# Two halves of a sparse attention result stored apart, and keys turned by DMA, in a one-core hybrid decoder layer

## The chip, the cores and the metric

The kernel runs on one core of a Trainium2 chip. The metric is the device time of one execution in microseconds (us); lower is better. A core has a matrix engine (PE, with its weight loader PEld), a vector engine (DVE), an engine for activations and copies (ACT), a general engine (POOL) and a queue (SP) from which this kernel issues all its transfers. Engines run side by side, each through its own instructions in order, and meet at semaphores.

## The reference, cut to what matters

One decoder layer over 1024 tokens of width 1024, float32:

```python
h = x @ w_in                                   # queries, keys, values, gates of both groups
o_diff = diff_attention(dq, dk, dv, ...)       # 4 heads, two softmaxes each, subtracted; RMS norm per head
o_nsa = gates[0]*o_cmp + gates[1]*o_sel + gates[2]*o_win   # 8 heads, sparse: compressed, selected, window
mix = concat([o_diff, o_nsa], -1) @ w_out
x = layer_norm(ALPHA * x + mix)
x = layer_norm(ALPHA * x + (silu(x @ w_gate) * (x @ w_up)) @ w_down)
```

Columns 0 to 511 of the concatenated row come from the differential heads, columns 512 to 1023 from the sparse heads.

## The kernel before

A float32 operand is kept as two tiles, a rounded part (hi) and a remainder (lo), and a product is three matmuls (`mm3`, L116 to L118). `split` (L81, L83) makes the pair: ACT copies, then DVE or POOL subtracts.

**Order of the work.** After the inputs and the first projections, attention runs in ten phases. A phase has units (a query block of 128 tokens of a pair of sparse heads, or of one differential head) and fillers (projections of the next queries, keys and values, and the first rows of the output projection) that are pumped between the units' steps. A unit has a `front` (scores with `scores`, L323 to L332; exponentials with `exps`, L346; gates on POOL, L411) and a `back` (transposes on PE, copies of them by ACT and DVE, products with the values into the one bank psO). The tile framework turns this into one fixed instruction order for each engine, the SP queue included, by priorities and modelled durations; it also adds the semaphores and gives out buffers: five tiles of the tag `w`, two banks psS, three psT, two psM, one psO.

**The end of a sparse unit.** For a block `i` and a head pair `p`, the selected and the window kind add into the same psO bank. Its upper 64 partitions hold the product with the values' hi, its lower 64 that with the values' lo. At the end of the window kind ACT copies the lower 64 to `tmp` (L433), DVE adds the upper 64 (L434), and two transfers (L436) store the two heads' 64x128 results to `mix_d[i]`, columns 4 to 7 of its eight column blocks. There are 32 such ends.

**Keys.** `k_fill` loads a 1024x128 weight, projects one half of the tokens at a time into a psM bank, and `evac_k` empties it: for each of the two heads in the bank, ACT writes hi to one half of the partitions (L170) and DVE writes lo to the other half (L171). This happens for ten halves beside attention, and for two halves ahead of it, from a psT bank. Queries are emptied by `evac_q` (L176, L177), after which three transfers inside SBUF (`move`, L161) copy partition halves.

**The output projection.** `out_start(i)` loads the residual row and the mix row `mix_d[i]`: `load_split_here` loads the sparse half (columns 512 to 1023) first, then the differential half, each to where lo will stand, and splits it (ACT, then DVE for rows 0 to 3, POOL for rows 4 to 7). A row takes two `w` tiles. `out_half` multiplies the sparse columns first, 24 matmuls for each half row and 48 in all; L605 adds the residual. Rows 0 to 3 are fillers of the last two phases; rows 4 to 7 stand behind attention, beside transposes (`x_put`, L913) for the feed-forward part, which takes the rest of the time and is not touched.

Of the kernel before, what the change touches and what calls it, by code (L numbers as in the profile page):

```python
# [11 lines left out]
F32 = mybir.dt.float32  # L12
# [5 lines left out]
P = 128  # L18
T = 1024
DM = 1024  # L20
NB = T // P
KT = DM // P
# [15 lines left out]
def layer_kernel(ctx: ExitStack, tc: tile.TileContext, xT, x, w_t, w_vg, w_dv, lam_in, subln,  # L38
# [4 lines left out]
    nc = tc.nc  # L43
# [5 lines left out]
    dram = ctx.enter_context(tc.tile_pool(name="dram", bufs=1, space=bass.MemoryType.DRAM))  # L49
# [7 lines left out]
    def ps_o():  # L57
        return psum.tile([P, 512], F32, tag="O", name="psO", bufs=1)
# [10 lines left out]
    def w_tile(dt=F32R):  # L69

        return slots.tile([P, 1024], dt, tag="w", name="w", bufs=5)

    mix_d = dram.tile([NB, P, KT, P], F32, name="mix_d")
    wo_d = dram.tile([2, 4, P, 1024], F32, name="wo_d")
    x1_d = dram.tile([NB, P, DM], F32, name="x1_d")
    a_d = dram.tile([NF // 2, 7, P, 512], F32, name="a_d")
# [2 lines left out]
    def split(src, hi, lo, l_eng="dve"):  # L79

        nc.scalar.copy(hi, src)  # L81
        eng = nc.vector if l_eng == "dve" else nc.gpsimd
        eng.tensor_sub(lo, src, hi.bitcast(F32))  # L83
# [9 lines left out]

    def load_split_here(src, hi, lo, l_eng="dve", order=(0,)):

        n = 1024 // len(order)
        for k in order:
            raw = lo[:, k * n:(k + 1) * n].bitcast(F32)
            nc.sync.dma_start(raw, src[:, k * n:(k + 1) * n])
            split(raw, hi[:, k * n:(k + 1) * n], lo[:, k * n:(k + 1) * n], l_eng)  # L100
        return hi, lo

    def w_tiles():
        lo = w_tile()
        return w_tile(), lo
# [38 lines left out]
    with ExitStack() as ctx_a:  # L144
        pa = ctx_a.enter_context(tc.tile_pool(name="pa", bufs=1))

        def small(shape, tag, bufs, dt=F32):
            return pa.tile(shape, dt, tag=tag, name=tag, bufs=bufs)
# [9 lines left out]
                    yield 0.33  # L158

        def move(dst, src):  # L160
            nc.sync.dma_start(dst.bitcast(F32), src.bitcast(F32))  # L161

        def evac_k(out):

            def f(hf, ps):
                cs = slice(hf * 512, (hf + 1) * 512)
                for g in range(2):
                    own = slice(g * 64, g * 64 + 64)
                    other = slice(64 - g * 64, 128 - g * 64)
                    nc.scalar.copy(out[g][own, cs], ps[own])  # L170
                    nc.vector.tensor_sub(out[g][other, cs], ps[own], out[g][own, cs].bitcast(F32))  # L171
            return f

        def evac_q(q, scale, ps):
# [120 lines left out]
        def q_of(qt, i, a):  # L295

            q = qt[1 + i // 4][a]
            c = (i % 4) * P
            return q[:, c:c + P], q[:, 512 + c:512 + c + P]
# [38 lines left out]
        def t_tiles(width):  # L338

            if width <= 512:  # L340
                t = pa.tile([P, 1024], F32, tag="t", name="t", bufs=6)
                return [t[:, 0:512], t[:, 512:1024]]
            return [pa.tile([P, 1024], F32, tag="t", name="t", bufs=6) for _ in range(2)]
# [31 lines left out]
        def nsa_units(p, qt, K, V):  # L375


            g = p // 2
            heads = (2 * p, 2 * p + 1)
            sl = [SLOPES[4 + h] for h in heads]  # L380
            state = {}

            def make(i, kind):
                nb = i + 1 if kind == 0 else min(i + 1, WIN_BLOCKS)
                j0 = i + 1 - nb
                width = nb * P
                ts = []

                def front():
                    dist = dsel[:, 1024 - width:] if kind == 0 else dwin[:, 640 - width:]  # L390
                    m = small([P, 4], "m", 4)
                    r = small([P, 4], "r", 4)
                    ts.extend(t_tiles(width))
                    if kind == 0:
                        pc = pa.tile([P, 2, NC], F32, tag="pc", name="pc", bufs=3)
                        ts.append(pc)
                    for a in range(2):
                        ms, rs = ([t[:, n:n + 1] for n in (a, 2 + a)] for t in (m, r))
                        cmp = (pc[:, a, :], dcmp[:, 56 - 8 * i:56 - 8 * i + NC], ms[1]) if kind == 0 else None
                        scores(q_of(qt, i, a), K[kind], j0 * P, width, dist, sl[a], ms[0], ts[a], cmp)  # L400
                        exps(ts[a], width, ms[0], rs[0])
                        if kind == 0:
                            exps(pc[:, a, :], NC, ms[1], rs[1])
                    nr = 2 if kind else 4
                    nc.vector.reciprocal(r[:, :nr], r[:, :nr])  # L405
                    for a in range(2):
                        for n, t in ((1 + kind, ts[a][:, :width]), (0, pc[:, a, :] if kind == 0 else None)):
                            if t is not None:
                                gc = heads[a] * 3 + n
                                c = a if n else 2 + a  # L410
                                nc.gpsimd.tensor_scalar(t, t, r[:, c:c + 1], gates[:, i, gc:gc + 1],  # L411
                                                        op0=ALU.mult, op1=ALU.mult)

                def back(fill):
                    if kind == 0:
                        state["po"] = po = ps_o()
                        ptc = transposed([ts[2][:, a, :] for a in range(2)], rows=64)
                        nc.tensor.matmul(po[:, :256], lhsT=vcc[g], rhs=ptc[:, 0, :256], start=True, stop=False)
                    po = state["po"]
                    for jj in range(0, nb, 2):  # L420
                        js = range(jj, min(jj + 2, nb))
                        pt = transposed([ts[a][:, j * P:(j + 1) * P] for j in js for a in range(2)])
                        for n, j in enumerate(js):
                            v = V[kind][:, (j0 + j) * P:(j0 + j + 1) * P]
                            last = kind == 1 and j == nb - 1
                            nc.tensor.matmul(po[:, :256], lhsT=v, rhs=pt[:, 0, n * 256:(n + 1) * 256],  # L426
                                             start=False, stop=False)
                            nc.tensor.matmul(po[:, :256], lhsT=v, rhs=pt[:, 1, n * 256:(n + 1) * 256],  # L428
                                             start=False, stop=last)
                        fill((jj + len(js)) / nb)  # L430
                    if kind == 1:
                        tmp = small([P, 256], "tmp", 3)[0:64, :]
                        nc.scalar.copy(tmp, po[64:128, :256])  # L433
                        nc.vector.tensor_add(tmp, po[0:64, :256], tmp)  # L434
                        for a in range(2):
                            nc.sync.dma_start(mix_d[i, a * 64:(a + 1) * 64, 4 + p, :], tmp[:, a * P:(a + 1) * P])  # L436

                return front, back, 2.0 * nb + 1

            return [make(i, kind) for i in range(NB) for kind in range(2)]  # L440
# [75 lines left out]
        def proj_steps(w, hf, done):  # L516

            ps = ps_m()
            for k in range(KT):
                ks = slice(k * P, (k + 1) * P)  # L520
                proj_mm3(ps, w[0][:, ks], w[1][:, ks], *x_at(k, hf * 512, 512), k == 0, k == KT - 1)
                yield 0.65
            done(hf, ps)

        def k_fill(n, where, out, halves=(0, 1)):
            def steps():
                if 0 in halves:
                    out.extend([slot(m) for m in where])
                    out.append(load_split(w_t[n], *w_tiles(), l_eng="pool", pieces=2))
                for hf in halves:  # L530
                    yield from proj_steps(out[2], hf, evac_k(out))
                    there.add((n, hf))
            return steps, 5.2 * len(halves)

# [52 lines left out]
        mix_rows = {}  # L587

        def out_start(i):

            acc[i] = slot((8, 9, 10, 11, 4, 2, 3, 5)[i], F32)
            nc.sync.dma_start(acc[i], x[i * P:(i + 1) * P, :])
            mix_rows[i] = load_split_here(mix_d[i].rearrange("p k t -> p (k t)"), *w_tiles(),
                                           "dve" if i < 4 else "pool", order=(1, 0))

        def out_half(i, nh, ps):
            m = mix_rows[i]
# [121 lines left out]
        for k0, nk in ((0, 3), (3, 3), (6, 2)):  # L719
            n = nk * 280  # L720
# [340 lines left out]
    for p in range(NF // 2):  # L1061
        f = 2 * p
        g = [gate_tile() for _ in range(2)]
        gate, up = gate_up(f, w_gate, f, half_tile(0)), gate_up(f + 1, w_up, f, half_tile(1))
# [129 lines left out]
    for j in range(4):  # L1194

        n = 2 if j == 3 else 1
        for c in range(n):
            cs = slice(c * 512 // n, (c + 1) * 512 // n)
# [5 lines left out]
            dst = acc[j + 4][:, cs]  # L1204
# [66 lines left out]
```

## Time and profile before

| | |
|---|---|
| median of 3 runs | 1304.74 us (1304.59 to 1304.9) |
| profiled execution, its own time | 1305.84 us |
| its span, first to last instruction | 1304.1 us |
| granted PE clock | 0.999 |
| transfers | 183.13 MB, mean 140 GB/s |

The 1.74 us between the profiled execution's time and its span lie outside the instructions. In the profile, "L434" is a line of the kernel; a row of a group gives engine, operation, what is written and read, shapes, the count, the busy time and the mean in ns. A PE matmul of 512 columns is shown for about 390 ns, but the next one starts about 230 ns later: matmuls overlap, and a full PE row hides waits of up to some 160 ns.

### The profile page before, as it was taken

To read this page: it belongs to the slowest core of one execution; us is meant where nothing else is said; L and a number is where in the kernel's file an instruction comes from. 1 tells how busy PE (TensorE), PEld (TensorE's weight loads), DVE (VectorE), ACT (ScalarE), POOL (GpSimd) and SP (SyncE) were. 2 spreads that over 40 slices of the span, in tenths; PEclk is the share of its full clock that TensorE was granted. 3 is DMA by queue.
4 is the path that set the end of the run, shared out by engine and by line. 5 is a ranking of instruction groups with operands and counts; after the bars stand their busy time and mean duration, and the time that the engine had idled before them with its cause. 6 is when DMAs were issued, how large, how long until landed. Compare 5 with 4: busy or idle time off the path is not lost.

```text
span 1304.1 us, 20490 instructions
## 1 busy us (share of the span) xinstructions
PE 1286.2 (99%) x6955; PEld 1107.8 (85%) x6955; DVE 917.8 (70%) x1963; ACT 652.1 (50%) x1398; POOL 464.1 (36%) x499
## 2 busy tenths in 40 slices
PE   9999999999999999999999999999999999999997
PEld 7998999988988889788887888888888888888886
DVE  5567867778778667774797677776766768555588
ACT  5366866868776566653353333333333335533330
POOL 4434534545435446643613313232231222000071
PEclk9999999999999999999999999999999999999999
DMA  9412012121112135623224566555555559768641
GB/s 354 132 31 62 22 35 62 49 48 48 35 55 70 50 94 149 218 82 113 81 76 149 180 232 228 194 178 173 174 170 185 187 179 346 259 200 291 195 168 65
DMA packets 86841, 183.13 MB, mean 140 GB/s; under 512 B 10576, under 2 KB 19152, under 8 KB 86608
## 3 DMA queue, kind: packets, MB, share of 16 engines
q1 hardware_dynamic: 86736, 181.82, 42.7%
q8 instruction: 55, 0.90, 0.3%
q14 instruction: 50, 0.41, 0.1%
HBM read 116.18 MB, written 57.15 MB: 133 GB/s over the span
## 4 chain that ended last, share of the span: by engine, by line
PE 91%; DVE 4%; DMA 2%; ACT 2%; issue 1%; POOL 0%; SPq 0%; DVEq 0%; ACTq 0%
PE psM L116 11%; PE psM L118 11%; PE psM L117 11%; PE psS L118 6%; PE psS L117 6%; PE psS L116 6%; PE psT L118 5%; PE psT L117 5%; PE psT L116 5%; PE psT L365 4%; PE psS L323 3%; PE psS L326 3%; PE psO L428 2%; PE psO L426 2%; PE psO L481 2%; PE psO L116 2%
## 5 line engine op out<-in xcount | busy, mean ns | idle before, releaser
L346 ACT ACTIVATE t<-t,m 128x384 f32<-128x384 f32 (+7 forms) x192 | 144.2, 752 | 65.4 <-DVE m L332 59.8
L411 POOL TENSOR_SCALAR t<-t,r,gates 128x640 f32<-128x640 f32 (+7 forms) x128 | 99.6, 783 | 180.5 <-DVE r L405 82.4
L116 PE MATMUL psM<-big,w 128*128 128x512 f32 x304 | 120.6, 397 | 0.6 <-DVE slot L171 0.3
L118 PE MATMUL psM<-big,w 128*128 128x512 f32 x304 | 120.1, 396 | 0.0
L117 PE MATMUL psM<-big,w 128*128 128x512 f32 x304 | 119.9, 394 | 0.0
L323 PE MATMUL psS<-slot,q 128*128 128x320 f32 (+10 forms) x304 | 111.8, 369 | 2.2 <-DVE m L332 2.0
L1019 POOL TENSOR_TENSOR half<-half,half 128x512 f32<-128x512 f32 x22 | 33.5, 1524 | 205.0 <-ACT half L1018 205.0
L83 DVE TENSOR_TENSOR pt<-psT,pt 128x512 fp32r<-128x512 f32 (+1 forms) x152 | 91.3, 615 | 13.1 <-ACT pt L81 11.7
L326 PE MATMUL psS<-slot,q 128*128 128x320 f32 (+10 forms) x304 | 99.5, 329 | 0.0
L81 ACT CAST pt<-psT 128x512 fp32r<-128x512 f32 (+1 forms) x152 | 77.3, 525 | 20.6 <-PE psT L365 10.0
L81 ACT CAST big<-slot 128x1024 fp32r<-128x1024 f32 (+1 forms) x54 | 54.4, 1018 | 66.2 <-DVE slot L1011 50.5
L83 DVE TENSOR_TENSOR op<-op 128x1024 fp32r<-128x1024 f32 x44 | 60.9, 1388 | 36.3 <-ACT op L81 35.8
L83 DVE TENSOR_TENSOR big<-slot,big 128x1024 fp32r<-128x1024 f32 (+1 forms) x54 | 63.5, 1182 | 30.5 <-ACT big L81 30.3
L365 PE MATMUL psT<-ident,t 128*128 128x128 f32 x528 | 83.8, 273 | 0.8 <-DVE pt L83 0.7
L81 ACT CAST op<-op 128x1024 fp32r<-128x1024 f32 x44 | 45.9, 1052 | 61.8 <-DMA op<-t_d 55.6
L428 PE MATMUL psO<-pt,slot 128*128 128x256 f32 x264 | 72.1, 294 | 0.1
L426 PE MATMUL psO<-pt,slot 128*128 128x256 f32 x264 | 71.8, 289 | 0.0
L332 DVE CUSTOM_DVE_ANT_0 t<-psS,dsel 128x384 f32<-128x384 f32 (+9 forms) x128 | 62.3, 493 | 13.4 <-PE psS L326 9.6
L1023 POOL TENSOR_TENSOR half<-half,half 128x512 f32<-128x512 f32 x22 | 36.5, 1659 | 99.0 <-DVE half L1022 98.8
L81 ACT CAST big<-big 128x1024 fp32r<-128x1024 f32 (+1 forms) x49 | 44.2, 912 | 45.6 <-DMA big<-t_d 34.0
L118 PEld LDWEIGHTS psM<-big,w 128*128 128x128 f32 x304 | 57.1, 188 | 11.4
L116 PEld LDWEIGHTS psM<-big,w 128*128 128x128 f32 x304 | 57.2, 188 | 11.1 <-ACT w L81 0.8
(371 smaller groups left out, 3971.3 us busy)
## 6 DMA issues: line engine op xcount, KB each, us to landing
a_d<-slot SPq DMA_DIRECT2D x77, 256.0 KB, 3.0
t_d<-slot SPq DMA_DIRECT2D x77, 256.0 KB, 2.2
q<-q SPq DMA_DIRECT2D x48, 256.0 KB, 2.9
slot<-in_w_up_dram SPq DMA_DIRECT2D x22, 512.0 KB, 3.8
slot<-in_w_down_dram SPq DMA_DIRECT2D x22, 512.0 KB, 3.9
op<-a_d SPq DMA_DIRECT2D x44, 256.0 KB, 3.5
op<-t_d SPq DMA_DIRECT2D x44, 256.0 KB, 4.0
big<-a_d SPq DMA_DIRECT2D x33, 256.0 KB, 2.9
```

Of the source, the lines that this page charges most:

```text
L81: nc.scalar.copy(hi, src)
L83: eng.tensor_sub(lo, src, hi.bitcast(F32))
L116: nc.tensor.matmul(acc, lhsT=ah, rhs=bh, start=first, stop=False, skip_group_check=more)
L117: nc.tensor.matmul(acc, lhsT=ah, rhs=bl, start=False, stop=False, skip_group_check=more)
L118: nc.tensor.matmul(acc, lhsT=al, rhs=bh, start=False, stop=last, skip_group_check=more)
L323: mm = nc.tensor.matmul(ps[:, :c + part], lhsT=q[0], rhs=k[:, ks], start=True, stop=False)
L326: nc.tensor.matmul(ps[:, :c + part], lhsT=q[1], rhs=k[:, ks], start=False, stop=True)
L346: nc.scalar.activation(t[:, :width], t[:, :width], AF.Exp, bias=m, scale=-1.0, accum_out=r)
L365: nc.tensor.transpose(tp[:rows, n * P:(n + 1) * P], s, ident)
L411: nc.gpsimd.tensor_scalar(t, t, r[:, c:c + 1], gates[:, i, gc:gc + 1], op0=ALU.mult, op1=ALU.mult)
L426: nc.tensor.matmul(po[:, :256], lhsT=v, rhs=pt[:, 0, n * 256:(n + 1) * 256], start=False, stop=False)
L428: nc.tensor.matmul(po[:, :256], lhsT=v, rhs=pt[:, 1, n * 256:(n + 1) * 256], start=False, stop=last)
```

## The change

Three edits.

1. At the end of a sparse unit ACT copies the whole psO bank (128 partitions) to `tmp`. The add is gone from this place. Two transfers store the two partition halves to a new DRAM tensor `mixs_d[i, n]`, one for the hi part and one for the lo part, each with both heads.
2. `out_start` loads the two stored halves into the two halves of a third `w` tile, adds them on POOL, and splits the sum into hi and lo. The differential half is loaded and split as before, from a `mix_d` that now has only four column blocks.
3. For keys beside attention, ACT copies the whole psM bank to the hi tile and DVE subtracts to the lo tile, 128 partitions each. Then three transfers exchange a quarter of each through a DRAM tensor `turn_d`, so that each head has its hi and its lo in one tile. The two halves ahead of attention keep `evac_k`.

```diff
-    mix_d = dram.tile([NB, P, KT, P], F32, name="mix_d")
+    mix_d = dram.tile([NB, P, 4, P], F32, name="mix_d")
+    mixs_d = dram.tile([NB, 2, P, 4, P], F32, name="mixs_d")
+    turn_d = dram.tile([5, 2, 64, 512], F32, name="turn_d")
...
+        def evac_k_whole(out, n):
+
+            def f(hf, ps):
+                cs = slice(hf * 512, (hf + 1) * 512)
+                nc.scalar.copy(out[0][:, cs], ps)
+                nc.vector.tensor_sub(out[1][:, cs], ps, out[0][:, cs].bitcast(F32))
+                up, down = out[1][0:64, cs], out[0][64:128, cs]
+                move(turn_d[n, hf], down)
+                move(down, up)
+                move(up, turn_d[n, hf])
+            return f
...
                     if kind == 1:
-                        tmp = small([P, 256], "tmp", 3)[0:64, :]
-                        nc.scalar.copy(tmp, po[64:128, :256])
-                        nc.vector.tensor_add(tmp, po[0:64, :256], tmp)
-                        for a in range(2):
-                            nc.sync.dma_start(mix_d[i, a * 64:(a + 1) * 64, 4 + p, :], tmp[:, a * P:(a + 1) * P])
+                        tmp = small([P, 256], "tmp", 3)
+                        nc.scalar.copy(tmp, po[:, :256])
+                        for n in range(2):
+                            nc.sync.dma_start(mixs_d[i, n, :, p, :].rearrange("(a e) t -> e a t", a=2),
+                                              tmp[n * 64:(n + 1) * 64, :].rearrange("e (a t) -> e a t", a=2))
...
-                    yield from proj_steps(out[2], hf, evac_k(out))
+                    yield from proj_steps(out[2], hf, evac_k_whole(out, (n - 9) // 2 if n > 3 else 4))
...
-            mix_rows[i] = load_split_here(mix_d[i].rearrange("p k t -> p (k t)"), *w_tiles(),
-                                           "dve" if i < 4 else "pool", order=(1, 0))
+            raw, m, l_eng = w_tile(F32), w_tiles(), "dve" if i < 4 else "pool"
+            parts = [raw[:, n * 512:(n + 1) * 512] for n in range(2)]
+            for n in range(2):
+                nc.sync.dma_start(parts[n], mixs_d[i, n].rearrange("p k t -> p (k t)"))
+            nc.gpsimd.tensor_add(parts[0], parts[0], parts[1])
+            split(parts[0], m[0][:, 512:1024], m[1][:, 512:1024], l_eng)
+            load_split_here(mix_d[i].rearrange("p k t -> p (k t)"), m[0][:, 0:512], m[1][:, 0:512], l_eng)
+            mix_rows[i] = m
```

More of the change, by code (lines that the diff above doesn't have):

```diff
@@ L94, in load_split_here @@
     def load_split_here(src, hi, lo, l_eng="dve", order=(0,)):
-        n = 1024 // len(order)
+        n = src.shape[-1] // len(order)
         for k in order:
@@ L160, in move @@
         def move(dst, src):
-            nc.sync.dma_start(dst.bitcast(F32), src.bitcast(F32))
+            nc.sync.dma_start(*(t if t.dtype == F32 else t.bitcast(F32) for t in (dst, src)))
         def evac_k(out):
```

## The prediction

> **What bounds the kernel now.** First the page: engine totals and the chain that ended last.
>
> ```profile
> span 1304.1 us, 20490 instructions
> PE 1286.2 (99%) x6955; PEld 1107.8 (85%) x6955; DVE 917.8 (70%) x1963; ACT 652.1 (50%) x1398; POOL 464.1 (36%) x499
> PE 91%; DVE 4%; DMA 2%; ACT 2%; issue 1%; POOL 0%; SPq 0%; DVEq 0%; ACTq 0%
> ```
>
> PE is the bound, and the change leaves its matmuls as they are. What can be won is PE's waiting, inside the stages that the change touches. Next, therefore, the busy times by stretches of 20 us. The first answer is of the six stretches of the sparse stage (100 to 420 us) in which PE is least full (its first and fifth row, and the sum), the second is the sum over the other ten of that stage, the third has the stretch of the first output rows and one of the last.
>
> ```profile
> 120.00:140.00 20.00, 19.14 (x127) 16.39 (x126) 18.03 (x65) 17.27 (x45) 11.59 (x14) 1.00 0.10 32
> ...
> 380.00:400.00 20.00, 19.07 (x141) 17.00 (x139) 18.35 (x61) 15.70 (x40) 8.53 (x11) 1.00 0.22 48
> ...
> sum 120.00, PE 116.25 PEld 104.23 DVE 104.04 ACT 95.83 POOL 62.84; mean PE 19.38 PEld 17.37 DVE 17.34 ACT 15.97 POOL 10.47
> ```
>
> ```profile
> sum 200.00, PE 199.95 PEld 184.98 DVE 138.81 ACT 141.07 POOL 85.38; mean PE 19.99 PEld 18.50 DVE 13.88 ACT 14.11 POOL 8.54
> ```
>
> ```profile
> 540.00:560.00 20.00, 17.75 (x116) 15.07 (x114) 15.78 (x47) 11.83 (x32) 8.86 (x9) 1.00 0.32 106
> ...
> 620.00:640.00 20.00, 20.00 (x96) 16.64 (x95) 13.79 (x21) 6.30 (x9) 14.17 (x11) 1.00 0.30 106
> ```
>
> PE's idle time in the sparse stage, 3.75 us of 120, is all in the stretches where DVE is busy 104.04 of 120 (87%). Where DVE is at 138.81 of 200 (69%), PE idles 0.05 us. So in that stage DVE, with ACT next (95.83), decides whether PE waits. Another 2.25 us of idle lie in 540 to 560; in the stretch behind attention there is none. PE's row is kind to waits, since its matmuls overlap, so the weight loader's waits of 100 to 420 us come next, and of the whole run the one on L171.
>
> ```profile
> PEld psS L323 <- DVE m L332: 4.0, 10, 1.0
> PEld psO L428 <- DVE pt L83: 2.0, 7, 0.4
> PEld psO L418 <- DVE pt L372: 1.1, 3, 0.5
> PEld psO L481 <- DVE tmp L434: 1.0, 1, 1.0
> ```
>
> ```profile
> PEld psM L116 <- DVE slot L171: 0.7, 2, 0.4
> ```
>
> All end with DVE. Two wait for the very lines that the change removes or shortens: 1.0 us for L434, 0.7 us for L171.
>
> **The change part by part.** The instructions that go or shrink, and DVE's time in L434 and in L171 inside the six tight stretches:
>
> ```profile
> L434 DVE TENSOR_TENSOR tmp<-psO,tmp 64x256 f32<-64x256 f32 x32 | 13.1, 410 | 8.7 <-ACT tmp L433 8.4
> L433 ACT COPY tmp<-psO 64x256 f32<-64x256 f32 x32 | 11.8, 369 | 8.8 <-PE psO L428 8.1
> L171 DVE TENSOR_TENSOR slot<-psM,slot 64x512 fp32r<-64x512 f32 x20 | 13.8, 689 | 1.4 <-ACT slot L170 0.8
> L170 ACT CAST slot<-psM 64x512 fp32r<-64x512 f32 x20 | 11.5, 580 | 2.9 <-DVE slot L171 1.8 <-PE psM L118 0.6 <-PE psS L326 0.4
> L81 ACT CAST pt<-psT 128x512 fp32r<-128x512 f32 x112 | 63.7, 581 | 16.0 <-PE psT L365 8.5 <-PE psO L418 5.5 <-DVE pt L83 0.8
> L83 DVE TENSOR_TENSOR pt<-psT,pt 128x512 fp32r<-128x512 f32 x112 | 75.3, 685 | 12.1 <-ACT pt L81 10.9
> ```
>
> ```profile
> sum 120.00, DVE 4.06; mean DVE 0.68
> ```
>
> ```profile
> sum 120.00, DVE 2.75; mean DVE 0.46
> ```
>
> *Sparse ends.* 32 adds go: 13.1 us of DVE, and 8.4 us in which DVE stood at its queue's head for ACT's copy. The copy stays at 369 ns: the rows L81 and L170 show 581 and 580 ns for 128 and 64 partitions, so the number of partitions costs nothing. psO comes free one DVE instruction earlier.
>
> *Key halves.* Ten halves lose one ACT copy (10 x 580 = 5.8 us) and one DVE subtraction (10 x 689 = 6.9 us); a whole tile costs 685 (L83). The psM bank comes free after one pair instead of two.
>
> What that is worth: the waits on L434 (1.0) go whole, since psO is then ACT's to free. Of the wait on L171 I take 0.5 of 0.7. The other DVE waits sum to 4.0 + 2.0 + 1.1 = 7.1 us. In the tight stretches DVE has 120 - 104.04 = 15.96 us free; removing 4.06 + 2.75/2 = 5.4 makes that 21.4. Letting the waits shrink as the free time grows gives 7.1 x (1 - 15.96/21.4) = 1.8 us. Bounds: 0 (ACT, 80% busy there, takes DVE's place) and all of 7.1. Gain in all 1.0 + 0.5 + 1.8 = 3.3 us, between 0 and 8.8.
>
> *Three more transfers for each key half*, 30 in all, one behind the other, on SP:
>
> ```profile
> q<-q SPq DMA_DIRECT2D x48, 256.0 KB, 2.9
> w<-mix_d SPq DMA_DIRECT2D x16, 256.0 KB, 2.8
> mix_d<-tmp SPq DMA_DIRECT2D x16, 128.0 KB, 2.8
> ```
>
> ```profile
> 448.24 0.69 DVE L171 TENSOR_TENSOR slot<-psM,slot 64x512 fp32r<-64x512 f32 x1
> ```
>
> ```profile
> 454.85 0.75 DVE L177 SCALAR_TENSOR_TENSOR q<-psM,qscale,q 128x512 fp32r<-128x512 f32 x1 [0.63 <-ACT q L176]
> ```
>
> ```profile
> 455.63 5.58 SPq L161 DMA_DIRECT2D q<-q  x3
> ```
>
> A store of 128 KB (2.8), a move inside SBUF (2.9) and a load (2.8): a key half is whole 8.5 us after DVE. It is nearest to use for head 2's first half: DVE ends at 448.93, so the key is there at 457.4. But that head's query needs its own three moves, issued from 455.63 to 461.21, the last landing 2.9 later, at 464.1. The query is the later one by 6.7 us. The other halves are used a phase or more after they are made, or, for head 3's first half, come ahead of their query as here. Price 0; without that cover 8.5 us per half. While SP waits for the first and the second of the three, what is queued behind (query moves, weight loads, stores of results) waits up to 2.8 + 2.9 = 5.7 us; only the query moves are near their use, and I take 0, at most 5.7 for one meeting at 455.
>
> *Stores of the sparse result.* Still two per end, of 64 KB instead of 32: at most the 2.8 us of a 128 KB store to land, and read only by the output rows, behind the whole sparse stage. 0; uncovered, 2.8 once.
>
> *Mix rows.* Each row gets one more load of 256 KB (2.8 us, beside the other) and a POOL add of 128x512, then the old split. POOL's price, what POOL does to DVE beside it, and the chain at the first rows:
>
> ```profile
> L934 POOL TENSOR_TENSOR slot<-slot,half x4: 1285/1290/1294, 638.8 to 666.5; 128x512 f32<-128x512 f32 x4
> ```
>
> ```profile
> L464 DVE SCALAR_TENSOR_TENSOR r<-r,lam,r x32: 207/220/1329, 395.1 to 583.4; 128x1 f32<-128x1 f32 x32
> ```
>
> ```profile
> 544.47 1.05 POOL ss L496
> ...
> 548.24 1.91 DMA mix_d<-tmp
> 550.15 0.02 issue
> 550.17 3.56 DMA w<-mix_d
> ```
>
> The wait at 540 to 560 belongs to the differential half of row 0, which the change leaves alone; but the chain passes POOL, where one add (1.29) may stand in front. Cost 0 to 1.29, taken 0.5. A DVE instruction of one column took between 207 and 1329 ns: some are held for up to 1.1 us. The Trainium skill has a reason (SBUF — State Buffer, section Who interferes with whom): a DVE instruction with two SBUF inputs and a POOL instruction that reads SBUF hold the same port by turns, and the second waits the first one out. By that rule the added POOL adds would each delay DVE, while L434, which reads one operand from PSUM, never disturbed POOL. The trace's 1329 ns agrees; what it would cost is the last rival.
>
> *The third w tile.* A row holds two tiles as before; the third is only needed until the split. Behind attention:
>
> ```profile
> 623.05 1.14 ACT L81 CAST w<-w 128x512 fp32r<-128x512 f32 x2
> ```
>
> ```profile
> 634.83 0.39 PE L116 MATMUL psS<-big,w 128*128 128x512 f32 x1
> ```
>
> Row 6 is split at 623.05, when row 4's tiles come free, and multiplied from 634.83: 11.8 us between. Should its load begin only at 623.05, it needs 2.8 + 1.29 + 1.14 + 1.29 (the POOL subtraction, as long as the add) = 6.5 us. It still fits. Price 0; without the cover 6.5 us a row.
>
> Sum: -3.3 + 0.5 = -2.8. The profiled execution's own 1305.84 (1304.1 of span and 1.74 around it) becomes 1303.0; it lies 1.1 above the median of 1304.74, from which the same sum gives 1301.9.
>
> **The rivals.** (1) *Hidden anyway.* ACT is at 95.83 of 120 in the tight stretches and gets next to nothing off; the waits pass from DVE to ACT, and only 1.0 + 0.5 - 0.5 is won: 1303.7. For it: ACT's 17.27 of 20 in the first tight stretch; against: ACT's 15.70 in the fifth, where PE is as idle.
> (2) *Slower: row loads exposed.* If the third tile makes the loads of a row begin when PE already needs it, PE stands for up to 6.5 us a row, since in 620 to 640 PE has no idle time to fill. It turns the sign from one row on (-2.8 + 6.5 = +3.7, 1308.4). Against it: the 11.8 us of cover.
> (3) *Slower: POOL holds DVE.* Four adds fall beside attention (rows 0 to 3); 1.1 us of DVE delay each is 4.4, and with 1.29 on the chain +5.7 - 3.3 = 2.4: 1307.1. It decides if all four lie where PE waits for DVE.
>
> **How the numbers follow.** A measurement of this kernel tells about 0.2%, 2.6 us, from no change. My forecast, a gain beyond 2.6, gets 0.43: the sum lies just past the mark and the waits leave room down to -8.8 (1295.9), and the instruction order is planned anew, which can go either way. Rival 1, with small moves either way, 0.37; rival 2, 0.13; rival 3, 0.07, half a step around the mark. Faster 0.43, same 0.37, slower 0.20. The range for 8 in 10 is 1297.5 to 1307.5: it leaves out the ends of the waits' bound and of exposed rows. For the forecast alone: 1297.5 to 1302.1.
>
> **What would show it.** Right: no DVE line in a sparse end, ACT's copy still near 369 ns; the six tight stretches with PE nearer 120 and DVE near 98; no loader wait on L434's successor; keys landed before the first scores of their head. Wrong: PE idle behind 600 us at the sparse columns of a row (rival 2); DVE instructions beside the POOL adds lasting over 1 us on the chain (rival 3); ACT in DVE's place among the loader's waits (rival 1); or new idle time at a phase's start, waiting for a key's third transfer.

## The result, and the profile after

The changed kernel took 1312.24 us (median; 1311.07 to 1313.73) against 1304.73 for the kernel before in the same comparison: 1.0054 times as long, with a 95% interval of 1.0039 to 1.0069. It is slower by some 7.5 us. The forecast was a gain of 2.8 us.

The head of the page after, in the order in which the lines of before were shown (span; engines; the chain that ended last):

```profile
span 1310.0 us, 20509 instructions
...
PE 1286.4 (98%) x6955; PEld 1109.7 (85%) x6955; DVE 899.3 (69%) x1921; ACT 641.7 (49%) x1388; POOL 472.6 (36%) x507
...
PE 88%; DVE 5%; DMA 2%; POOL 2%; issue 1%; ACT 1%; DVEq 0%; SPq 0%; POOLq 0%; ACTq 0%
```

The 32 adds, the ten copies and the ten subtractions are gone: DVE has 18.5 us less, ACT 10.4 less, and PE has the same 1286 us. The span is 5.9 us longer all the same, so PE waits more. Two milestones say how far attention has come: the last sparse end (the ACT copy of psO, last start) and the last product of attention. The first two lines are of before, the last two of after; of interest is the second of the two start times.

```profile
L433 ACT COPY tmp<-psO x32: 368/369/373, 86.8 to 407.5; 64x256 f32<-64x256 f32 x32
L481 PE MATMUL psO<-slot,pt x288: 270/275/378, 409.4 to 600.4; 128*128 128x128 f32 x144
```

```profile
L447 ACT COPY tmp<-psO x32: 349/372/382, 86.3 to 405.7; 128x256 f32<-128x256 f32 x32
L495 PE MATMUL psO<-slot,pt x288: 270/275/415, 406.2 to 607.0; 128*128 128x128 f32 x144
```

At the end of the sparse stage the changed kernel is 1.8 us ahead (405.7 against 407.5; it was 0.5 ahead at the first end already). At the end of attention it is 6.6 us behind (607.0 against 600.4). So attention falls back by 8.4 us between the two, beside the differential units, where the change adds no work but the adds and loads of four rows and some key transfers. The busy times of PE by stretches (before, then after; the first number behind the stretch's length is PE's busy time, and DVE's is the third):

```profile
60.00:420.00 360.00, 356.20 (x2433) 326.45 (x2432) 268.24 (x955) 262.06 (x732) 161.15 (x228) 1.00 0.19 47
...
480.00:600.00 120.00, 116.98 (x722) 102.44 (x721) 82.27 (x222) 70.91 (x183) 64.87 (x65) 1.00 0.47 141
600.00:700.00 100.00, 98.77 (x493) 81.80 (x492) 75.81 (x115) 41.36 (x71) 38.53 (x28) 1.00 0.27 95
```

```profile
60.00:420.00 360.00, 355.41 (x2445) 327.79 (x2444) 254.64 (x920) 255.05 (x730) 161.59 (x229) 1.00 0.24 59
...
480.00:600.00 120.00, 112.79 (x678) 98.54 (x677) 77.14 (x217) 67.18 (x174) 70.26 (x68) 0.99 0.51 154
600.00:700.00 100.00, 97.82 (x496) 80.79 (x495) 73.91 (x112) 41.67 (x71) 42.42 (x34) 1.00 0.32 102
```

In 60 to 420 PE idles 4.6 us instead of 3.8, but has begun 12 matmuls more. In 480 to 600 it idles 7.2 us instead of 3.0, though every engine but POOL is busy for less of that time; in 600 to 700 it idles 2.2 instead of 1.2. The 0.8, 4.2 and 1.0 us more of idle time come to 6.0, about the 5.9 by which the span grew, so the loss of time is mostly in 480 to 600. It is smaller than the 8.4 us by which attention falls back, since the milestones also move with the fillers between them: in the run h3 below, which takes as long as the kernel before, the last product starts at 596.9 instead of 600.4.

The sparse stage shows what became of the forecast gain. The loader's waits there (100 to 420 us) in after, of which L323 and L337, L418 and L432, L428 and L442 are the same lines before and after:

```profile
PEld psO L432 <- DVE pt L386: 3.2, 4, 1.6
PEld psS L337 <- DVE m L346: 3.1, 5, 0.9
PEld psO L442 <- DVE pt L85: 1.9, 7, 0.4
```

The wait on the add is gone, but these three sum to 8.2 us, where the four on DVE before, with that one, had 8.1. DVE's free time did not become shorter waits.

What PE waits for in 480 to 600, from its own waits in after:

```profile
PE psS L337 <- DMA q<-q: 2.3, 1, 2.3
PE psT L514 <- DVE od L511: 1.6, 1, 1.6
PE psS L337 <- DVE m L346: 1.5, 1, 1.5
```

None of these is an operation that the change put in: a query's move inside SBUF, the norm of a finished row block, and a row maximum. The first wait has a second price. Behind it the matmuls of 256 columns start 0.21 us apart instead of 0.12, and the granted clock stands at one half for 3.4 us; the stretch 500 to 510 shows it as 0.83 in the column behind POOL's:

```profile
504.93 0.41 PE L337 MATMUL psS<-slot,q 128*128 128x128 f32 x1 [2.26 <-DMA q<-q]
...
506.32 0.41 PE L119 MATMUL psM<-slot,big 128*128 128x256 f32 x1
506.53 0.41 PE L120 MATMUL psM<-slot,big 128*128 128x256 f32 x1
```

```profile
500.00:510.00 10.00, 7.74 (x52) 7.53 (x52) 8.10 (x25) 4.89 (x18) 7.65 (x9) 0.83 0.71 211
```

### The profile page after: what moved, and what is told of

Its sections match the earlier page's. It is cut to its first block, busy times and chain, and to the rows that moved or that the text cites. A ratio compares the mean times of both kernels' runs of the same rounds, so it can differ in the third digit from the quotient of the medians.

```text
span 1310.0 us, 20509 instructions
## 1 busy us (share of the span) xinstructions
PE 1286.4 (98%) x6955; PEld 1109.7 (85%) x6955; DVE 899.3 (69%) x1921; ACT 641.7 (49%) x1388; POOL 472.6 (36%) x507
## 4 chain that ended last, share of the span: by engine, by line
PE 88%; DVE 5%; DMA 2%; POOL 2%; issue 1%; ACT 1%; DVEq 0%; SPq 0%; POOLq 0%; ACTq 0%
PE psM L118 10%; PE psM L120 10%; PE psM L119 10%; PE psT L120 5%; PE psT L118 5%; PE psT L119 5%; PE psS L120 5%; PE psS L119 5%; PE psS L118 5%; PE psT L379 5%; PE psS L337 3%; PE psS L340 3%; PE psO L442 2%; PE psO L440 2%; PE psO L495 2%; PE psO L120 2%
## 5 line engine op out<-in xcount | busy, mean ns | idle before, releaser
L337 PE MATMUL psS<-slot,q 128*128 128x320 f32 (+10 forms) x304 | 111.4, 368 | 5.9 <-DVE m L346 3.2
L442 PE MATMUL psO<-pt,slot 128*128 128x256 f32 x264 | 72.3, 295 | 0.1
L346 DVE CUSTOM_DVE_ANT_0 t<-psS,dsel,m 128x384 f32<-128x384 f32 (+7 forms) x80 | 50.2, 628 | 29.3 <-PE psS L340 27.3
L337 PEld LDWEIGHTS psS<-slot,q 128*128 128x128 f32 x304 | 57.7, 190 | 12.7 <-DVE m L346 5.9
```

Source lines behind the costliest of these rows:

```text
L337: mm = nc.tensor.matmul(ps[:, :c + part], lhsT=q[0], rhs=k[:, ks], start=True, stop=False)
L346: nc.vector.tensor_tensor_reduce(out=t[:, at:at + part], in0=ps[:, c:c + part], in1=dist[:, at:at + part], scale=slope, scalar=3.0e38 if h ...
```

## The experiments

Times are medians beside the kernel before of the same comparison, which stood at 1304.9 to 1305.4; the ratio to it and its 95% interval stand in brackets. The expectations write TensorE, VectorE, ScalarE and GpSimd for PE, DVE, ACT and POOL.

**First: which edit?** Theory K, formed from the wait on `q<-q`: the three transfers of head 3's keys hold the queue, so the weights of w_out and the query's moves come late. The rival: edits 1 and 2 (sparse ends and rows).

*e1_rows*: edits 1 and 2, keys as before.

```diff
-                yield from proj_steps(out[2], hf, evac_k_whole(out, ...))
+                yield from proj_steps(out[2], hf, evac_k(out))
```

> Edits 1 and 2 alone (sparse halves stored apart, added on POOL at the mix row); all keys are emptied as before. Theory K (head 3's key exchange on SP holds back the w_out loads and the query moves behind it at 479 to 505 us): no key transfers, so no 2.4 us wait of PE on a query move near 502, no drop of the PE clock there; 1303 to 1305. Rival M (the mix rows: POOL adds and the third w tile cost the time, at 530 to 560): most of the loss stays, 1309 to 1313. Rival P (any newly planned order costs some us here): somewhere between, with waits of PE in other places.

*e2_keys*: the kernel before with edit 3 alone.

> Edit 3 alone (whole-tile keys with the exchange by transfers); the sparse end and the mix rows as before. Theory K: the loss stays, 1308 to 1313, with PE waiting for a query move near 500 us behind w_out loads. Rival M: 1302 to 1304.5, since the waits on L171 are shorter and nothing else changes. Rival P: waits in other places.

*e3_head3_old*: the changed kernel, but head 3's keys emptied the old way (`evac_k(out) if n == 15 else ...`).

> The changed kernel, but the two key halves of differential head 3 (the last, beside the first loads of w_out) are emptied as before, without exchange; the other eight keep it. Theory K: only these six transfers collide, so 1303 to 1306.5 and no query wait near 500. Rival M: 1309 to 1313. Rival P: in between.

*e4_head3_only*: the kernel before, with head 3's keys alone emptied the new way.

> The kernel before, with only the two key halves of differential head 3 emptied whole and exchanged by transfers. Theory K: these six transfers alone cost 3 to 7 us, 1308 to 1312, with PE waiting for a query move near 500. Rival M: 1304 to 1305. Rival P: a change of 0 to 3 us either way.

Measured: e1 1314.45 (ratio 1.0067, interval 1.0054 to 1.0080); e2 1303.83 (0.9988, 0.9979 to 0.9997); e3 1311.63 (1.0043, 1.0029 to 1.0056); e4 1305.38 (1.0000, 0.9992 to 1.0009). Theory K fell. With head 3's keys as before, PE still waits 2.0 us for a query's move at the same place and most of the loss stays (6.4 us); put into the kernel before, those keys cost nothing. The new keys as a whole gain 1.4 us, and e2 is the one version here that beats both kernels. Edits 1 and 2 lose 9.2.

**Second: ends or rows, and by which operation?** *f1_ends*: edit 1 alone; a row loads only the first stored half, so the second half is left out of the result.

```diff
...
-            nc.gpsimd.tensor_add(parts[0], parts[0], parts[1])
-            split(parts[0], m[0][:, 512:1024], m[1][:, 512:1024], l_eng)
...
+            load_split_here(mixs_d[i, 0]..., m[0][:, 512:1024], m[1][:, 512:1024], l_eng)
```

> Edit 1 alone: the sparse ends store two halves, but a mix row loads only the first of them straight to its place, with two w tiles and no POOL add, as before (the second half is left out of the result). Keys as before. The two edits on the sparse result together cost 9 us. Theory R (the mix row is dear: POOL add, third tile, later split): 1300 to 1305. Rival S (the sparse end is dear: without its add the planned order of the sparse stage becomes worse; the first kernel with both edits lost 2.7 us more between 102 and 415 us than the kernel before): 1307 to 1313.

*f2_rows*: edit 2 alone; the end adds on DVE as before and stores one sum, which the row loads twice and adds on POOL (the sparse half comes out doubled).

> Edit 2 alone: the sparse ends add and store one result as before; a mix row loads it twice into a third w tile, adds the two on POOL and splits the sum (the sparse half of the row comes out doubled). Keys as before. Theory R: 1310 to 1315, with waits of PE from 480 us on. Rival S: 1304 to 1306.

*f3_dve*: edits 1 and 2, with a row's add on DVE (`nc.vector.tensor_add`).

> Edits 1 and 2, keys as before, the mix row's add on DVE instead of POOL. If POOL's add is what costs (it holds POOL for 1.3 us a row in front of the differential units' work, and DVE beside it): 1303 to 1308. If it is the third w tile: 1312 to 1316, unchanged. Rival S: unchanged too.

*f4_two_tiles*: edits 1 and 2 without the third `w` tile: the raw halves are loaded into the residual's tile, and x is loaded there after the split.

> Edits 1 and 2, keys as before, without the third w tile: the two stored halves are loaded into the row's residual tile, added there on POOL and split from there, and the residual row is loaded behind the split. If the third tile is what costs (buffers of w come free later, and the row's loads with them): 1303 to 1308. If POOL's add: 1312 to 1316. Rival S: unchanged, 1312 to 1316.

Measured: f1 1309.22 (1.0034, 1.0022 to 1.0046); f2 1310.68 (1.0047, 1.0035 to 1.0060); f3 1313.20 (1.0061, 1.0049 to 1.0074); f4 1313.89 (1.0066, 1.0054 to 1.0079). Each edit loses by itself (4.3 and 5.8 us). Neither POOL as the place of the add nor the third tile explains the pair: with each taken away in turn, 8 to 9 us stay lost, against 9.2 with both (e1).

**Third: the operation, or the order that the planner makes of it?** Edit 1 does less work and yet loses. *g1_no_add* is the kernel before with nothing but the 32 adds taken out (the upper half of each result is left out):

```diff
                         nc.scalar.copy(tmp, po[64:128, :256])
-                        nc.vector.tensor_add(tmp, po[0:64, :256], tmp)
```

> The kernel before with only the 32 additions of VectorE at the ends of the sparse units taken out: ScalarE copies the lower half of the bank as before, and the two old stores write that copy (the upper half of each result is left out); row loads, keys and stores stay. The instructions of TensorE, VectorE and GpSimd then stand in exactly the order of f1_ends (966 lines of TensorE's differ from the kernel before), while the stores and the queue are nearly the old ones. Theory O (the cost of the ends is the order that the planner makes once psO is modelled free some 0.4 us earlier): 1309 us as f1_ends, within 1.5, and the products again wait at the copies of the transposed tiles. Theory S (the cost is the wide stores of two halves, or the queue that issues them): 1304 to 1305, as before or a little less for the additions. My chances: O 0.75, S 0.2.

*g2_stores* has the old end with its add, and the stores of f1 (the whole sum in both halves; the row loads the first):

```diff
                         nc.vector.tensor_add(tmp, po[0:64, :256], tmp)
+                        for n in range(2):
+                            nc.sync.dma_start(mixs_d[i, n, :, p, :]..., tmp...)
```

> The old end with its addition on VectorE, but the stores of f1_ends: both halves of the new buffer are written, each with the whole sum, and a mix row loads the first of them directly. TensorE, VectorE and GpSimd then have exactly the order of the kernel before; 50 lines of the queue differ. Theory O: 1304.9, as before, within 1.5. Theory S: 1309, as f1_ends. Also the row load by two pieces of 512 from two buffers is in here without a third tile and without an addition: if it is a part of the cost of f2_rows it shows as up to 5.8 us. My chances: O 0.75, S 0.15.

*g3_rows_no_add* is f2 without POOL's add.

```diff
-            nc.gpsimd.tensor_add(parts[0], parts[0], parts[1])
```

> f2_rows without the addition on GpSimd: the stored sum is loaded twice into a third tile of tag w, but only the first load is split into the row; what the row lacks is the doubling. Theory T (the third tile and the second load make the row late or fill the five tiles): 1310.7, as f2_rows. Theory A (the addition, with the place that it takes in GpSimd's order ahead of the w_out subtractions and the row split that waits for it): 1305 to 1306. In between (1307 to 1309) if the planner's order is touched by both: 81 lines of TensorE's order still differ from before, where f2_rows has 149. My chances: A 0.5, between 0.3, T 0.2.

*g4_rows_wo_dve* is f2 with the subtractions of w_out's split on DVE (`l_eng="dve"` in `wo_fill`).

> f2_rows with the 16 subtractions that split w_out (128x512 each, 8 tiles of two halves) moved from GpSimd to VectorE. Theory P (in f2_rows VectorE's small instructions of the row statistics and the pow on GpSimd, which stands among these subtractions, fall into the stretch 527 to 536 us in which GpSimd subtracts, and each is held 0.8 to 1.0 us, 2.65 us in all, which TensorE waits out once at the scores of the last window): the wait of TensorE on the row maximum there falls from 4.8 to about 1 us, and the time to about 1307 to 1308. Rival: VectorE's 16 subtractions of about 0.6 us each stand in front of its small instructions instead and cost as much or more: 1310 to 1312. My chances: P 0.5, rival 0.35, else 0.15.

Measured: g1 1309.15 (1.0032, 1.0020 to 1.0043), g2 1305.38 (1.0002, 0.9993 to 1.0010). Theory O holds for the ends as far as its forecasts go: the wide stores cost nothing, and taking out 32 instructions, with nothing else in the program changed, costs 4.1 us. In g1 the sparse stage and the loader's waits in it (100 to 420 us) read:

```profile
60.00:420.00 360.00, 353.60 (x2411) 323.60 (x2411) 256.95 (x919) 260.05 (x727) 159.32 (x226) 1.00 0.19 47
```

```profile
PEld psO L428 <- DVE pt L83: 3.6, 12, 0.5
PEld psO L418 <- DVE pt L372: 3.1, 4, 1.8
PEld psO L426 <- ACT pt L81: 1.1, 3, 0.7
```

DVE has 11.3 us less to do than before (268.24 in the same stretch), and PE idles 6.4 us instead of 3.8. The wait of 1.0 us on the add is gone, as forecast. In its place the products wait for the copies of their transposed tiles: 7.8 us in these three rows, where the kernel before had 3.4, the two rows shown with the prediction (2.0 and 1.1) and

```profile
PEld psO L426 <- ACT pt L81: 0.3, 1, 0.3
```

The stretch 480 to 600 adds 1.5 us of idle time (PE is busy 115.49 of 120 there, 116.98 before). With psO modelled free one instruction earlier, the planner puts products ahead of matmuls that used to stand before them (966 lines of PE's order differ), and they come to wait for their copies. That the old order would have kept g1 from losing is argued, not measured: no run has the old order without the adds.

g3 took 1306.66 (1.0010, 1.0002 to 1.0019), g4 1310.98 (1.0043, 1.0030 to 1.0055). Of the 5.8 us of f2, the second load and the third tile have 1.7 (0.2 to 2.5 by the interval); the rest, some 4, came with POOL's add. The hold-up on DVE that I had read in f2's trace is real. Here are the scaling of a row block and the one-column instruction of L478, first f2, with POOL's subtractions beside them, then g4, where those are gone and POOL stands idle:

```profile
531.43 4.20 POOL L85 TENSOR_TENSOR big<-big 128x512 fp32r<-128x512 f32 x3
...
531.80 1.45 DVE L511 TENSOR_TENSOR od<-od,ss 128x512 f32<-128x512 f32 x1
533.18 1.24 DVE L478 SCALAR_TENSOR_TENSOR r<-r,lam,r 128x1 f32<-128x1 f32 x1
```

```profile
537.23 0.68 DVE L511 TENSOR_TENSOR od<-od,ss 128x512 f32<-128x512 f32 x1
537.84 0.21 DVE L478 SCALAR_TENSOR_TENSOR r<-r,lam,r 128x1 f32<-128x1 f32 x1
```

So the rule of the Trainium skill (SBUF — State Buffer, section Who interferes with whom) agrees with the trace: 1.45 and 1.24 us beside POOL's subtractions, 0.68 and 0.21 without. But the time did not come back: DVE's own subtractions then stand ahead of these two instructions, which start at 537 instead of 532. Theory P, that this hold-up is what f2 loses, got no support. What f2 and the changed kernel share is where the casts of w_out stand in ACT's order. ACT in the kernel before, then in after, then in e3; in brackets the idle time ahead of an instruction:

```profile
524.01 0.83 ACT L346 ACTIVATE t<-t,m 128x640 f32<-128x640 f32 x1 [0.23 <-DVE ss L495]
...
524.84 0.82 ACT L346 ACTIVATE t<-t,m 128x640 f32<-128x640 f32 x1
...
528.48 0.62 ACT L81 CAST big<-big 128x512 fp32r<-128x512 f32 x1 [2.73 <-DMA big<-wo_d]
```

```profile
529.20 0.62 ACT L83 CAST big<-big 128x512 fp32r<-128x512 f32 x1 [5.25 <-DMA big<-wo_d]
529.73 0.83 ACT L360 ACTIVATE t<-t,m 128x640 f32<-128x640 f32 x1
...
533.44 0.84 ACT L360 ACTIVATE t<-t,m 128x640 f32<-128x640 f32 x1
```

```profile
525.74 0.82 ACT L360 ACTIVATE t<-t,m 128x640 f32<-128x640 f32 x1
...
527.48 1.24 ACT L83 CAST big<-big 128x512 fp32r<-128x512 f32 x2 [0.83 <-DMA big<-wo_d]
```

Before, both exponentials of the unit (640 columns) stand ahead of the first cast that waits for its load. After, both stand behind it, and ACT idles 5.25 us in front of them. In f2 the second one does (it starts at 530.28, the first cast at 526.75). But e3 has both ahead, as before (they start at 524.90 and 525.74), and loses 6.4 us all the same; so have e1 and f4, which lose 9.2 and 9.0. The place of the exponentials is therefore not what these kernels lose by, or not alone.

**Fourth: does any new order cost as much?** Only the planner's constants are changed; the work is the same. *h1_before_pace* and *h2_after_pace*:

```diff
-                yield 0.65
+                yield 0.7
```

> The kernel before with the same work and another order: the cost with which the planner counts one step of a value projection or of the output rows is 0.7 instead of 0.65, so fillers are spread a little thinner between the steps of attention (897 lines of TensorE's order differ, against 1329 between the kernel before and the changed one). Theory L (any new order of this work loses some microseconds against the one of the kernel before): 1307 to 1311. Theory M (the edits cost by what they are: psO free earlier pulls products tight behind their copies, and the addition of a row sets back the scores beside it; another order as such is harmless): 1304 to 1306. My chances: L 0.55, M 0.35, faster than 1303.5 0.1.

> The changed kernel with the same constant (0.7 for 0.65; 847 lines of TensorE's order differ from the changed kernel's). Theory L: anywhere between 1304 and 1312, as likely under 1309 as over it, since the order is drawn anew. Theory M: 1310 to 1313, as the changed kernel, because what it does to psO and to the rows is still there. My chances: under 1308.5 0.4, 1308.5 to 1313.5 0.5, more 0.1.

*h3_before_ahead* and *h4_after_ahead*, in the ninth phase only:

```diff
-             [wo_fill(0), qdf(3, 1), wo_fill(1), ...], 2, 1.25, 40, None),
+             [wo_fill(0), qdf(3, 1), wo_fill(1), ...], 2, 1.2, 40, None),
```

> The kernel before, where fillers run ahead of attention by 1.2 instead of 1.25 in the ninth phase only (the last but one, with w_out and the first output rows): 123 lines of TensorE's order differ, all between about 480 and 600 us, where f2_rows has 103 of its own. Theory L: 1306 to 1310, lost in that stretch alone, the sparse stage as before. Theory M: 1304 to 1305.5. My chances: L 0.5, M 0.4, faster 0.1.

> The changed kernel with the same constant (1.2 for 1.25 in the ninth phase; 85 lines of TensorE's order differ, all between about 480 and 605 us). Theory L: the stretch beside w_out, which lost some 6.6 us of TensorE against the kernel before, comes out otherwise: between 1306 and 1312, and the spell of half clock at 505 may be gone. Theory M: 1311 to 1313. My chances: under 1310 0.45, 1310 to 1313.5 0.45, more 0.1.

Measured: h1 1309.39 (1.0032, 1.0020 to 1.0043); h2 1314.63 (1.0072, 1.0058 to 1.0085); h3 1305.27 (1.0001, 0.9993 to 1.0010); h4 1313.16 (1.0062, 1.0050 to 1.0075). A new order alone can cost the kernel before as much as edit 1 did, 4.4 us, and in the same stage: in h1 it shows

```profile
60.00:420.00 360.00, 353.14 (x2410) 323.58 (x2409) 266.28 (x949) 260.59 (x727) 160.01 (x226) 1.00 0.19 47
```

```profile
PEld psO L418 <- DVE pt L372: 3.2, 4, 1.5
PEld psO L428 <- DVE pt L83: 2.2, 5, 0.8
```

with PE idle for 6.9 us and the same line L418 waiting 3.2 us (1.1 before), although no instruction was added or taken out. Another new order (h3) cost nothing. So neither theory as I had put it holds: not any order costs, and not only these edits do. Nor did the changed kernel get better when its order was drawn anew; two draws are too few to say that it cannot.

**Fifth: the late load of w_out.** *i1_after_x_late* and *i2_keys_x_late*, the second on top of e2: the rows' x loads wait until w_out's second half has begun to be split.

```diff
+            nc.gpsimd.tensor_copy(acc[i][:, 0:1], wo[1, 0][1][:, 0:1].bitcast(F32))
             nc.sync.dma_start(acc[i], x[i * P:(i + 1) * P, :])
```

> The changed kernel, where the load of each input row x for the output rows has to wait for the first split tile of the second half of w_out (one column of it is copied into the row's tile by GpSimd before the load, which then overwrites it), so on the queue w_out's second half (8 x 256 KB) goes ahead of the rows (512 KB each) instead of behind four of them; 223 lines of TensorE's order differ from the changed kernel's. Theory D (the late load of w_out holds ScalarE at its cast with the exponentials of the unit behind it): the idle time of ScalarE at that cast falls from 5.25 us to under 2 us, and the time by 2 to 4 us, to 1308 to 1310.5. Rival R (the place of the scores in TensorE's own order decides, whatever the load does): 1311 to 1314. My chances: D 0.5, R 0.4, else 0.1.

> The kernel before with the new keys alone (e2_keys, 1303.83 us), and the same late loads of the input rows; 33 lines of TensorE's order differ from those of e2_keys. Theory D: ScalarE's wait of 2.7 us at the first cast goes, but little of TensorE waits for it there, so 1302.5 to 1304. Rival: rows that now arrive later, or GpSimd's copies in between, cost something: 1304.5 to 1307. Either way it tells whether a version with the keys can be had that beats both kernels by more than 0.1%. My chances: D 0.55, rival 0.35, under 1302.5 0.1.

Measured: i1 1310.58 (1.0047, 1.0033 to 1.0061), i2 1308.37 (1.0023, 1.0014 to 1.0032). In i1 the first cast came 3 us earlier, but ACT still idled 3.65 us ahead of it, where theory D had forecast under 2, so i1 tests it only in part:

```profile
526.18 0.62 ACT L83 CAST big<-big 128x512 fp32r<-128x512 f32 x1 [3.65 <-DMA big<-wo_d]
```

The half clock is gone and the median is 1.7 us below the changed kernel's, but the intervals overlap: not settled. i2 lost 4.5 us against e2 (3.0 against the kernel before), more than either theory had forecast. The postponed x loads fell on a query's moves, which took 11.2 us to land, and PE stood for them. In e2, whose first four x loads are issued some 10 us earlier, the same moves took 3.9 (first e2's moves, then in i2 the transfers issued in 528 to 532, then PE in i2):

```profile
q<-q SPq DMA_DIRECT2D x3, 256.0 KB, 3.9
```

```profile
slot<-in_x_dram SPq DMA_DIRECT2D x2, 512.0 KB, 10.9
q<-q SPq DMA_DIRECT2D x2, 256.0 KB, 11.2
```

```profile
546.16 0.60 PE L336 MATMUL psS<-slot,q 128*128 128x320 f32 x1 [4.17 <-DMA q<-q]
```

## Why the prediction was wrong, step by step

- **The waits on DVE shrink as its free time grows (1.0 + 0.5 + 1.8 of gain): this step failed.** It held the order of the instructions fixed and let the removed work turn into earlier starts. DVE's time did go down as counted, and the wait on L434 went whole. But the order is made anew from modelled durations, and in it PE's products came to stand closer to their copies. In the changed kernel the waits on DVE in the sparse stage sum to 8.2 us instead of 8.1 and PE idles 4.6 us instead of 3.8, so nothing of the 3.3 shows there as less waiting; with edit 1's adds alone taken out (g1), 3.4 us of waits on copies became 7.8 and the kernel lost 4.1.
- **The price of the rows (0.5 for POOL's add, 0 for the third tile and the second load): this step failed too, and the changed kernel's loss lies in its stage.** Edit 2 alone cost 5.8 us (f2), and of the 6.0 us more that PE idles in the changed kernel 5.2 come behind 480 us. The two bullets on it below have the parts.
- *What the two share.* The prediction did write that "the instruction order is planned anew, which can go either way", and gave that no price, no place and no rival. A new order of unchanged work cost 4.4 us in h1 and nothing in h3. The direction, slower, was among its rivals (0.20), but by other mechanisms.
- *The ACT copy does not grow with the partitions*: right, 372 ns at the median for 128 against 369 for 64.
- *Stores of the sparse result, 0*: right (g2, within 0.1%).
- *Keys, exchange at no price, a gain of about 1*: the size was right. 1.4 us gained (e2, which also has an order of its own), and no wait of PE on a key's transfer in after. A meeting on the queue, for which I allowed up to 5.7 us, was not it either: e1 has no exchange at all and loses 9.2 us, and e3 kept the wait on the query's move without head 3's exchange.
- *POOL's add in a row, 0.5, at most 1.29*: mis-sized. f2 against g3 is 1310.68 against 1306.66, some 4 us. An add of 1.3 us does not last that long, and its order differs from g3's too; which of the two costs is not shown. f3, with the add on DVE, is no faster than e1 beyond the noise (1313.20 and 1314.45), so it isn't POOL as such.
- *The third w tile and the second load, 0*: mis-sized, 1.7 us (g3; 0.2 to 2.5 by the interval). The place was the one of rival 2, behind attention: PE idles 2.2 us in 600 to 700 instead of 1.2, and in g3 as well. It is 1 us in all, not 6.5 a row.
- *Rival 3, POOL holds DVE*: the hold-up is there (1.24 us for a one-column instruction), its price is not shown; g4 took it from these instructions and stayed at 1311.
- *The sum*: in the changed kernel the sparse stage did end 1.8 us earlier, and attention falls back only behind it. But with the old keys the same ends and rows (e1) bring the last sparse end to 410.0, 2.5 us later than before. The parts do not keep their prices when they are put together, so the 4.3 of f1 and the 5.8 of f2 are not shares of the 7.5 us. What in after's own order costs the time behind the sparse stage is settled only in part: 2.3 us of a late query's move and the half clock behind it (3.4 us at half speed are 1.7). The rest, and why the move comes late, stay open.

## What to carry to other kernels

Where a planner makes the order from modelled times, an edit is two edits, one to the work and one to the order, and the second can be the larger: price it first by re-planning the same work (here 0 and 4.4 us), and run a part of the edit that keeps the old order (g2) or one that brings the new order with little else (g1) before an operation is blamed. Removing instructions from an engine that is not the bound can cost time: 32 adds fewer on DVE, 4.1 us more. A milestone of one stage moves with the fillers around it; count the idle time of the bound engine as well. And look for a pattern that two slow kernels share, here the late exponentials, in the other slow ones before it is blamed.

## What the runs showed of the hardware

- Behind one wait of PE of 2.26 us the granted clock stood at one half for 3.4 us (matmuls of 256 columns 0.21 us apart instead of 0.12). The Trainium skill (TensorE: Matmul & The Clock Gate, Part 1) gives about 3.4 us without work for that; here a shorter wait stood before it. Its length alone does not decide: a wait of 2.04 us in e3 (to 503.7) was not followed by half clock, one of 1.83 us in f3 (to 516.5) was.
- The 11.2 us landing in i2: the same 256 KB moves inside SBUF took 3.9 us in e2, where no 512 KB loads of x were issued beside them.
- An ACT copy of 256 columns took 372 ns at the median for 128 partitions and 369 for 64.
